# Weight and activation tiles begun 0 to 24 bytes inside buffers that are 32 bytes longer

## Chip, core and metric

The kernel runs on one core of one Trainium2 chip. The metric is the device time of one execution in microseconds (us), the median over runs. Before the change it is 1123.51 us, the median of three runs between 1121.23 and 1124.25 us.

## The reference

A trunk of two layers over 512 tokens of width 1024, all in float32. Layer 0 mixes tokens by stick-breaking attention (16 heads of 64), layer 1 by a gated MLP over chunks of 128 tokens; each is followed by a SwiGLU feed-forward of width 2816, and each of the four sub-layers is wrapped in RMSNorm before and after, with shift, scale and gate from a conditioning vector `c`.

```python
for i in range(DEPTH):                                   # 2 layers
    shift, scale, gate = ada_modulation(c, mix_ada_w[i], mix_ada_b[i])
    h = rms_norm(x, mix_pre_g[i]) * (1.0 + scale) + shift
    y = stick_breaking_mixer(...) if i == 0 else token_mixing_mixer(...)
    x = x + gate * rms_norm(y, mix_post_g[i])
    shift, scale, gate = ada_modulation(c, ffn_ada_w[i], ffn_ada_b[i])
    h = rms_norm(x, ffn_pre_g[i]) * (1.0 + scale) + shift
    y = (silu(h @ w_gate) * (h @ w_up)) @ w_down
    x = x + gate * rms_norm(y, ffn_post_g[i])
```

Nearly all of the arithmetic is dense matrix products with 1024 or 2816 rows of weights.

## The kernel before, in words

**Products.** Every float32 operand is split into a high part, rounded to the matmul format `float32r`, and a low part, the rest. A product is then three matmuls (`mm3`, lines 101 to 104): high by high, low by high, high by low. The split takes one ScalarE instruction (high) and one VectorE instruction (low); `split` is lines 109 to 114. All matmuls go through line 90, the transposes through line 98. Each matmul instruction shows in the profile twice: as a weight load (PEld, the stationary operand, 128 columns) and as the matmul (PE, the moving operand, 256 or 512 columns in nearly all of them, 128 in the transposes and the spatial gating).

**Which operand is which.** In the q/k projections, the u half of the gated MLP's input (`u`), and the gate and up products (`gu`, `r`) the weights are stationary (`wh`, `wl`) and the activations move (`hTh`, `hTl`, `Sh`, `Sl`). In the v projections (`v`), the output projections and the down products (`y`, `X`, `M`) the activations are stationary and the weights move.

**Gate and up.** Of the 22 blocks of 128 feed-forward columns, the first three run as plain products (`gu`), the other 19 by a scheme with seven half-size products in place of eight (`seven`, banks `r1` to `r3`), for which VectorE forms sums of weights (`f13`, `f24`) and of activations (`S`). The last down product does the same for part of its blocks (`M`, `X`).

**Where the tiles lie.** Two helpers hand out most of the buffers.

- `slot` (line 47) takes one of 28 buffers of 4,096 bytes per partition from the pool `s4`. Transposed activations, queries, keys, attention outputs, split activations, modulation rows, the rows of `x` that are loaded again, and some modulation weights (`rawada` where `slots=True`) all live there.
- `wtile` (line 151) takes a pair of buffers, `wh` and `wl`, from the pool `wpool`, with five buffers of 4,096 bytes for each, and later in turn from a sixth pair in `wpool2`.

Counted from the start of a partition, the pools lie one after the other in the order in which they are opened: the five `wh` buffers begin at byte 10,528 + 4,096 n, the five `wl` buffers at 31,008 + 4,096 n, the 28 slots at 65,088 + 4,096 n, and the sixth pair at 187,968 and 192,064. So, within 64 bytes, the ten buffers of `wpool` all begin at byte 32, and all slots and the sixth pair at byte 0; the unpadded buffers of the second weight block (`b21`) begin at byte 0 as well. The slices of them that a matmul reads lie at multiples of 512 bytes, which changes nothing in that. A tile's *phase* below is its start within 64 bytes. The raw weights land in buffers of another pool (`wraw`, `wraw2`), which are not touched by the change.

**Order.** The weights come as a written list (`stream`): each is loaded by SyncE's DMA queue, split, and used in that order. In the attention and in the first stage TensorE, VectorE and ScalarE are chained to the order in which the program writes their instructions; elsewhere a scheduler orders them by dependencies. Buffers are handed out as earlier tiles are released.

**Numbers of names.** `nm` (line 43) counts up one number for each name it makes; a tile's name ends in it.

Of the kernel before, what the change touches and what calls it, by code (L numbers as in the profile page):

```python
# [9 lines left out]
F32R = mybir.dt.float32r  # L10
# [3 lines left out]
P = 128  # L14
# [11 lines left out]
def trunk(ctx: ExitStack, tc: tile.TileContext, A: dict, out: bass.AP):  # L26
# [8 lines left out]
    s4 = ctx.enter_context(tc.tile_pool(name="s4", bufs=28))  # L35
# [3 lines left out]
    uid = [0]  # L39
# [3 lines left out]
    def nm(s):  # L43
        uid[0] += 1
        return f"{s}_{uid[0]}"

    def slot(dt, name, a=2, b=512):
        return s4.tile([P, a, b], dt, tag="s4", name=nm(name))

    def bank(name, tag="b"):  # L50
        return psum.tile([P, 512], F32, tag=tag, bufs=6 if tag == "b" else 2, name=nm(name))
# [82 lines left out]
    def wemit():  # L134
        n = len(got)
        src, a, b, key = stream[n]
        if len(raws) == n:
            wload()
        if src is None:
            if len(raws) == n + 1 < len(stream) and stream[n + 1][0] is None:  # L140
                wload()
            got.append(blocks(*raws[n]))
            return
        raw = raws[n]
        if dve.chain and len(raws) == n + 1 and stream[n + 1][0] is not None:
            wload()
        h, l = wtile(a, b)
        split(h[:], l[:], raw[:])
        got.append((h, l))

    def wtile(a, b):
        turn[0] = (turn[0] + 1) % sum(c for _, c in wpools)
        pool = wpools[0][0] if turn[0] < wpools[0][1] else wpools[1][0]
        return (
            pool.tile([P, a, b], F32R, tag="wh", name=nm("wh")),
            pool.tile([P, a, b], F32R, tag="wl", name=nm("wl")),
        )

    def block_loads(idx):
# [10 lines left out]
    def blocks(xr, yr):  # L170

        fp = fwork["pool"]
        x = wtile(KD, P)
        split(x[0][:], x[1][:], xr[:])
        b21 = [fp.tile([P, 4, P], F32R, tag=f"b21{i}", name=nm("b21")) for i in range(2)]
        split(b21[0][:], b21[1][:], yr[:, 0:4, :])
        f13 = fp.tile([P, KD, P], F32, tag="f13", name=nm("f13"))
        add = dve.tensor_tensor(
            f13[:].rearrange("p (a k) f -> p a (k f)", a=2),
            xr[:].rearrange("p (a k) f -> p a (k f)", a=2),  # L180
            yr[:, 4:8, :].rearrange("p (a k) f -> p a (k f)", a=1).to_broadcast([P, 2, 512]),
            ALU.add,
        )
        order(add, ready[0])
        t13 = wtile(KD, P)
        split(t13[0][:], t13[1][:], f13[:])
        f24 = fp.tile([P, KD, P], F32, tag="f24", bufs=1, name=nm("f24"))
        dve.tensor_tensor(f24[:, 0:4, :], f13[:, 0:4, :], xr[:, 4:8, :], ALU.add)
        dve.tensor_tensor(f24[:, 4:8, :], f24[:, 0:4, :], yr[:, 0:4, :], ALU.add)
        t24 = wtile(KD, P)  # L190
        split(t24[0][:], t24[1][:], f24[:])

        def half(t, i):
            return lambda k: (t[0][:, 4 * i + k, :], t[1][:, 4 * i + k, :])

        return {
            "B11": half(x, 0), "B22": half(x, 1), "B21": half(b21, 0),
            "T1": half(t13, 0), "T3": half(t13, 1), "T2": half(t24, 0), "T4": half(t24, 1),
        }
# [82 lines left out]
    cT, ident = pack[:, :KD], pack[:, KD : KD + P]  # L282
    cols = pack[:, KD + P :].rearrange("p (a b) -> p a b", a=2)
    x0 = [slot(F32, "x0", 1, 1024)[:, 0, :] for _ in range(NT)]
    for tt, xt in enumerate(x0):
        load(xt, A["x"][tt * P : (tt + 1) * P, :])
# [26 lines left out]
    class Bg:  # L313
# [24 lines left out]
        def run(self):  # L338
            for name, at, s, part in self.parts:
                acc = slot(F32, name, 1, D)[:, 0, :]  # L340
                ada[name, at] = acc
                nc.gpsimd.memset(acc, 0.0)
                load(acc[0:1, :], A["adab"][s, part], self.queue)
                for k in range(KD):
                    if self.slots:
                        raw = slot(F32, "rawada", 1, D)[:, 0, :]
                        load(raw, A["ada"][s, part, k])
                        yield
                    else:
                        self.ahead(1 + (k + 1 < KD or name != self.parts[-1][0]))  # L350
                        raw = self.raws.pop(0)
                    ada_stt(acc, raw, k)
                    if not self.slots:
                        yield
# [1171 lines left out]
```

## Time and profile before

| | |
|---|---|
| median of three runs | 1123.51 us (1121.23 to 1124.25) |
| the profiled execution: span from first to last instruction | 1122.0 us; its time around the span is not recorded apart |
| busy TensorE matmul / weight load | 1104.4 us / 993.9 us |
| busy VectorE / ScalarE / GpSimd | 903.3 / 603.4 / 39.8 us |
| matmuls | 7,318 |
| granted TensorE clock, mean | 0.995 |
| moved by DMA | 176.09 MB, 157 GB/s on average |

Durations of matmuls in the profile overlap: a new one starts before the one ahead of it has ended. What a matmul costs in a stretch without gaps is therefore not its duration but the time from its start to the next start, which this text calls its *step*.

### The profile page before, as it was taken

The page shows a single profiled execution, that of the slowest core. Times are in us where ns is not written, and L with a number is a line of the kernel's source. Part 1 is how long each engine was busy: PE and PEld are TensorE (multiplying, and loading weights), DVE is VectorE, ACT ScalarE, POOL GpSimd, SP SyncE. Part 2 cuts the span into 40 slices and gives each one's busy share as a digit, 9 for nine tenths or more (in the row PEclk, how much of TensorE's full clock was granted, in tenths as well). Part 3 has the DMA queues.
Part 4 walks back from the last instruction along what each step waited for, and adds up shares of the span by engine and source line. Part 5 has one row for each costly group of instructions (what it writes and reads, how often), then busy time and mean ns, then how long its engine had stood idle before and what let it go on. Part 6 is the DMA issues. An engine that isn't in the chain of part 4 may idle for free.

```text
span 1122.0 us, 18286 instructions
## 1 busy us (share of the span) xinstructions
PE 1104.4 (98%) x7318; PEld 993.9 (89%) x7318; DVE 903.3 (81%) x1161; ACT 603.4 (54%) x977; POOL 39.8 (4%) x71
## 2 busy tenths in 40 slices
PE   6999999999999999999999999999999999999997
PEld 5788878779999999988878988989999999989896
DVE  7777889759998988797587774759988988889986
ACT  7646767646655555552244634437555555556552
POOL 0220111000000000010000000000000000000000
PEclk9999999999999999999999999999999999999999
DMA  9676445353344444278874582333244444223223
GB/s 358 229 228 169 142 147 160 135 188 132 106 125 147 151 148 122 90 243 264 272 255 167 182 286 80 110 129 134 77 151 140 128 133 147 76 75 113 95 96 149
DMA packets 51298, 176.09 MB, mean 157 GB/s; under 512 B 5643, under 2 KB 6155, under 8 KB 50318
## 3 DMA queue, kind: packets, MB, share of 16 engines
q1 hardware_dynamic: 45166, 153.95, 42.0%
q0 software_dynamic: 6048, 20.98, 6.0%
q8 instruction: 57, 0.93, 0.3%
q14 instruction: 27, 0.22, 0.1%
HBM read 164.43 MB, written 8.39 MB: 154 GB/s over the span
## 4 chain that ended last, share of the span: by engine, by line
PE 88%; DMA 6%; DVE 3%; ACT 2%; issue 1%; SPq 0%; DVEq 0%; ACTq 0%
PE r L90 33%; PE y L90 12%; PE X L90 7%; PE v L90 7%; PE pqk L90 7%; PE gu L90 6%; PE u L90 4%; DMA rawada<-in_ada 3%; PE M L90 3%; PE z L90 2%; PE av L90 2%; PE tw L98 2%; DMA raw<-in_wdown 1%; DMA ada<-in_ada0w 1%; PE tp L98 1%; PE sv L90 1%
## 5 line engine op out<-in xcount | busy, mean ns | idle before, releaser
L64 ACT ACTIVATE wh<-raw 128x1024 fp32r<-128x1024 f32 (+1 forms) x112 | 117.0, 1051 | 138.3 <-PE y L90 45.6
L64 DVE TENSOR_TENSOR wl<-raw,wh 128x1024 fp32r<-128x1024 f32 (+1 forms) x112 | 135.0, 1211 | 59.4 <-ACT wh L64 57.9
L90 PE MATMUL r<-Sh,wh 128*128 128x256 f32 x608 | 170.2, 280 | 0.3 <-ACT e L64 0.3
L90 PE MATMUL r<-Sh,wl 128*128 128x256 f32 x608 | 170.4, 280 | 0.0
L90 PE MATMUL r<-Sl,wh 128*128 128x256 f32 x608 | 170.1, 280 | 0.0
L90 PE MATMUL y<-wh,as 128*128 128x512 f32 x480 | 154.0, 398 | 0.0
L64 DVE TENSOR_TENSOR wl<-f,wh 128x1024 fp32r<-128x1024 f32 x76 | 92.8, 1220 | 35.8 <-ACT wh L64 35.8
L64 ACT ACTIVATE wh<-f 128x1024 fp32r<-128x1024 f32 x76 | 80.7, 1061 | 67.9 <-PE r L90 64.8
L90 PEld LDWEIGHTS r<-Sh,wh 128*128 128x128 f32 x608 | 114.7, 189 | 0.5 <-ACT e L64 0.5
L90 PEld LDWEIGHTS r<-Sl,wh 128*128 128x128 f32 x608 | 114.6, 189 | 0.0
L90 PEld LDWEIGHTS r<-Sh,wl 128*128 128x128 f32 x608 | 114.6, 189 | 0.0
L90 PEld LDWEIGHTS y<-wh,as 128*128 128x128 f32 x480 | 90.7, 189 | 21.3
L90 PE MATMUL y<-wl,as 128*128 128x512 f32 x240 | 95.5, 398 | 0.0
L90 PE MATMUL r<-hTh,wh 128*128 128x256 f32 x304 | 88.8, 293 | 0.0
L90 PE MATMUL r<-hTl,wh 128*128 128x256 f32 x304 | 84.8, 279 | 0.0
L90 PE MATMUL r<-hTh,wl 128*128 128x256 f32 x304 | 80.1, 280 | 0.0
L90 PE MATMUL X<-wh,as 128*128 128x512 f32 (+1 forms) x272 | 76.2, 356 | 0.0
L64 ACT ACTIVATE e<-r 128x256 f32<-128x256 f32 x114 | 43.4, 382 | 51.9 <-PE r L90 51.7
L90 PEld LDWEIGHTS r<-hTh,wh 128*128 128x128 f32 x304 | 57.2, 188 | 5.1 <-DVE gu L64 0.9
L90 PE MATMUL r<-hTh,b 128*128 128x256 f32 x304 | 60.7, 282 | 0.0
L64 ACT ACTIVATE wh<-rawx 128x1024 fp32r<-128x1024 f32 x38 | 40.4, 1062 | 36.5 <-PE r L90 30.8
L90 PEld LDWEIGHTS r<-hTl,wh 128*128 128x128 f32 x304 | 57.3, 188 | 0.1
(240 smaller groups left out, 2842.6 us busy)
## 6 DMA issues: line engine op xcount, KB each, us to landing
rawada<-in_ada SPq DMA_DIRECT2D x56, 512.0 KB, 4.7
raw<-in_wdown SPq DMA_DIRECT2D x44, 512.0 KB, 4.0
rawy<-in_wy SPq DMA_DIRECT2D x38, 512.0 KB, 3.6
rawx<-in_wx SPq DMA_DIRECT2D x38, 512.0 KB, 4.3
rawada<-in_ada POOLq DMA_DIRECT2D x24, 512.0 KB, 4.5
raw<-in_wqk SPq DMA_DIRECT2D x16, 512.0 KB, 4.2
ada<-in_ada0w SPq DMA_DIRECT2D x7, 1026.0 KB, 11.2
raw<-in_wgu SPq DMA_DIRECT2D x12, 512.0 KB, 3.5
```

Source lines behind the costliest of these rows:

```text
L64: b = f(*a, **k)
L90: b = nc.tensor.matmul(o, l, r, start=start, stop=stop, skip_group_check=True)
L98: last_tp[0] = nc.tensor.transpose(o, i, ident)
```

## The change

Each buffer of `slot` and `wtile` gets 8 more float32 elements (32 bytes) per partition, and the tile begins `o` elements inside it, where `o` is 0, 2, 4 or 6 by a formula on the name's number. Nothing else is edited; the instructions, their shapes and their written order are the same.

```diff
+    PAD = 8
+
+    def shifted(pool, a, b, dt, tag, name):
+        t = pool.tile([P, a * b + PAD], dt, tag=tag, name=nm(name))
+        o = uid[0] * uid[0] // 3 % 4 * 2
+        return t[:, o : o + a * b].rearrange("p (a b) -> p a b", a=a)
+
     def slot(dt, name, a=2, b=512):
-        return s4.tile([P, a, b], dt, tag="s4", name=nm(name))
+        return shifted(s4, a, b, dt, "s4", name)
...
         return (
-            pool.tile([P, a, b], F32R, tag="wh", name=nm("wh")),
-            pool.tile([P, a, b], F32R, tag="wl", name=nm("wl")),
+            shifted(pool, a, b, F32R, "wh", "wh"),
+            shifted(pool, a, b, F32R, "wl", "wl"),
         )
```

Two things follow from the arithmetic alone. For a number u, `u * u // 3 % 4` depends only on u modulo 6 and is 0, 0, 1, 3, 1, 0: half of the tiles begin at byte 0 of their buffer, a third at byte 8, a sixth at byte 24, and none at byte 16. And buffers of 4,128 bytes no longer begin at the same phase: neighbours in a pool differ by 32 within 64 bytes, whatever `o` is.

## The prediction

> **What bounds the kernel now.** I read the clock first, then the busy shares, the chain that ended last, the stages, and at last the starts of single matmuls, because the change edits nothing but addresses.
>
> ```profile
> core 0: 1122.0 us, clock 0.995
> ```
> ```profile
> span 1122.0 us, 18286 instructions
> ...
> PE 1104.4 (98%) x7318; PEld 993.9 (89%) x7318; DVE 903.3 (81%) x1161; ACT 603.4 (54%) x977; POOL 39.8 (4%) x71
> ...
> PE 88%; DMA 6%; DVE 3%; ACT 2%; issue 1%; SPq 0%; DVEq 0%; ACTq 0%
> ```
>
> The clock is granted in full, matmuls are busy for 98% of the span, and 88% of the chain that ended last is TensorE. So the time is the sum of the matmuls' steps, plus some gaps. The span of 1122.0 us is 1.5 us below the median of 1123.51 and inside the three runs; I make the sum as a difference and take it from the median.
>
> ```profile
> core 0: us, PE busy (x) PEld busy (x) DVE busy (x) ACT busy (x) POOL busy (x), PEclk, DMA share, GB/s
> 296.00:480.00 184.00, 184.00 (x1536) 181.72 (x1535) 156.48 (x211) 98.97 (x166) 0.96 (x1) 1.00 0.41 130
> 480.00:580.00 100.00, 97.99 (x449) 80.14 (x448) 78.42 (x84) 37.76 (x56) 2.87 (x3) 0.98 0.81 263
> ```
>
> In the stage of the seven products VectorE is busy for 156.48 of 184 us, 85%: TensorE could go some per cent faster there before VectorE held it. From 480 to 580 us it is otherwise; a chain of loads of modulation weights, here its first and last, paces the end:
>
> ```profile
> 492.50 5.99 DMA rawada<-in_ada
> ...
> 544.21 4.88 DMA rawada<-in_ada
> ```
> ```profile
> PE adaps L90 <- ACT acch L64: 2.0, 1, 2.0
> ```
>
> TensorE waits there once, 2.0 us, for a row that hangs on those loads. What it gains ahead of that wait is given back.
>
> **Does a matmul's step depend on where its operands lie?** Four stretches without gaps, each by its first and last row or as one piece of the chain. The first has moving tiles at phase 0 and weights at phase 32 (256 columns), the second both at phase 0.
>
> ```profile
> 400.18 0.28 PE L90 MATMUL r<-Sl,wh 128*128 128x256 f32 x1
> 400.30 0.28 PE L90 MATMUL r<-Sh,wl 128*128 128x256 f32 x1
> 400.42 0.28 PE L90 MATMUL r<-Sh,wh 128*128 128x256 f32 x1
> 400.53 0.28 PE L90 MATMUL r<-Sl,wh 128*128 128x256 f32 x1
> ...
> 402.98 0.28 PE L90 MATMUL r<-Sl,wh 128*128 128x256 f32 x1
> ```
> ```profile
> 410.11 0.28 PE L90 MATMUL r<-Sh,wh 128*128 128x256 f32 x1
> ...
> 411.07 0.28 PE L90 MATMUL r<-Sh,wl 128*128 128x256 f32 x1
> ```
>
> 24 steps in 2.80 us are 116.7 ns; 8 steps in 0.96 us are 120.0 ns. These are the same products of the same block, and only the pair of weight buffers differs (`wpool`, then `wpool2`). Unrounded, the first stretch repeats 120, 113, 116, 117 ns, the second has 120 every time. Now 512 columns, first weights moving at phase 32 over activations at phase 0, then both at phase 0:
>
> ```profile
> 649.75 19.60 PE v L90 x84
> ```
> ```profile
> 999.22 0.62 PE L90 MATMUL X<-wh,as 128*128 128x512 f32 x2
> ...
> 1003.99 0.39 PE L90 MATMUL X<-wh,as 128*128 128x512 f32 x1
> ```
>
> 19.60/84 = 233.3 ns, against 21 steps in 4.77 us, 227.1 ns. So it does depend, and the two widths disagree: equal phases cost a 256-column matmul about 3 ns more, and a 512-column matmul 6 ns less. What runs beside each matmul is the weight load of the next, so I read this as two streams of reads that get in each other's way or don't, by their distance within 64 bytes.
>
> [...]
>
> **The change part by part.** Over the whole trace, the starts give 4,559 gapless steps of 256 columns with a mean of 117.7 ns (1,204 pairs at equal phases, 3,355 at 32 apart), and 1,948 of 512 columns with a mean of 232.7 ns (265 equal, 1,683 apart). Some of the groups they come from:
>
> ```profile
> L90 PE MATMUL r<-Sh,wl 128*128 128x256 f32 x608 | 170.4, 280 | 0.0
> L90 PE MATMUL y<-wh,as 128*128 128x512 f32 x480 | 154.0, 398 | 0.0
> ```
>
> Now both lengths change. Working out the new starts from the pools, with buffers taken in the same order as now, the distance between moving and stationary tile becomes: for 256 columns 20% equal, 19% 32 apart, 61% at 8, 16 or 24 either way; for 512 columns 18%, 15% and 67%. Most pairs get distances that this trace doesn't show.
>
> Bounds for those: below, the best step seen, 113.3 (the low one of the repeating four, 113 or 114) and 227.1; above, the worst seen, 120.0 and about 235 (the upper ones within the 84 above). Between them I take the middle. For 256 columns the repeating 120, 113, 116, 117 helps: these steps pass through different relative positions of the two streams, and their mean is 116.7, the middle of 113.3 and 120. Equal phases look like one position held for good, at the worst value. With distances that change from matmul to matmul nothing is held, so I expect the mean over positions: **256 columns: 116.7 − 117.7 = −1.0 ns, by 4,559 = −4.4 us.** For 512 columns the middle of 227.1 and 233.3 is 230.2: **230.2 − 232.7 = −2.5 ns, by 1,948 = −4.9 us.** Of these some 244 lie in the paced stretch (57 us from 492 to 549, at 233.3 ns each) and give back 244 × 2.5 ns = 0.6 us. Sum: −4.4 − 4.9 + 0.6 = **−8.7 us**.
>
> The other engines read and write the shifted tiles too. For VectorE the trace has a row: half of these sixteen have their input and output begun 8 bytes off a multiple of 32 (the second of two rows of 1,026 elements).
>
> ```profile
> L64 DVE SCALAR_TENSOR_TENSOR ada<-ada,scr x16: 1217/1220/1230, 10.9 to 45.3; 128x1026 f32<-128x1026 f32 x16
> ```
>
> Shortest to longest is 1217 to 1230 ns, so the shift costs VectorE at most 13 ns in 1,220, about 1%, and I take nothing: that would be lost in the 15% that it has free. ScalarE has no such row; at VectorE's 1% its 603.4 us grow by 6, and with 54% busy they lie beside matmuls. The loads into slots may pay for rows begun off 32 bytes. Two loads of 513 KB (one of them begun 8 bytes off) stand beside one of 512 KB in the same first 20 us:
>
> ```profile
> ada<-in_ada0w SPq DMA_DIRECT2D x2, 513.0 KB, 8.8
> ...
> raw<-in_wv SPq DMA_DIRECT2D x1, 512.0 KB, 9.4
> ```
>
> Not slower, so nothing for those either. If they did cost more, the cover is that slots are loaded ahead, except the last rows of `x`; none of the wide weight loads lands in a shifted buffer. No wait, no instruction and no queue position is added.
>
> **Where it lands.** 1123.5 − 8.7 = 1114.8 us. A measurement here can tell about 0.3% (3.4 us) from no change.
>
> **The rivals.**
>
> *No change.* Either new distances count in proportion between the two known points, or addresses matter little for other reasons. In proportion, 256 columns would cost the mean of 120.0 and 116.7, 118.35: +0.65 ns, +3.0 us; with −4.9 + 0.6 that is −1.3 us, **1122.2**. For it: the two widths react with opposite signs, so that a random mix cancels. Against it: the repeating four, whose mean is lower than such a mix.
>
> *Slower: a tile begun inside a 32-byte piece costs a further piece.* The steps 113.3, 116.7 and 120 lie 3.3 ns apart, eight columns of 4 bytes at this rate: as if the streams came in pieces of 32 bytes. A row that begins 8 or 24 bytes inside one touches one more. Where the 256-column step is held by weight load and moving stream alike (PEld 181.72 busy in 184), a shift of either would add 3.3 ns: 3,282 pairs have one, 10.8 us; for 512 columns only the moving one, 1,065 pairs, 3.5 us. −8.7 + 14.3 = +5.6 us, **1129.1**; on the proportional sum −1.3 + 14.3 = +13.0 us, 1136.5. It decides the sign from 8.7/14.3, some 60% of that price. For it: the even spacing of the steps. Against it: VectorE's row, which pays nothing for the same shift.
>
> [...]
>
> *Much faster: the streams hardly ever meet.* If 32 bytes and 0 are special because tiles at multiples of 32 fall into step, and everything else runs at the best step seen, 256 columns win 4.4 ns × 4,559 = 20 us and 512 columns 5.6 × 1,948 = 10.9 us: −30 us, 1093; half of it, since 40% of the pairs stay at 0 or 32, is about 1105. For it: 113 ns is reached, one time in four. Against it: no stretch holds it.
>
> **How the numbers follow.** The forecast (mean over positions) gets 0.42, no change 0.24, slower 0.24, much faster 0.10. The range reaches up between the two slower sums, to 1132, and down past the half of the best case, to 1101: outside lie most of what is left of the full best case and of the slower case on the proportional sum. Faster by over 0.3%: 0.42 + 0.10 = 0.52; within: 0.24; slower: 0.24.
>
> **What would show it.** In the changed kernel, the count and the durations of VectorE's and ScalarE's groups stay as they are, and the difference is in the steps alone. Right: `v`, `y` and `X` stretches at 228 to 232 ns instead of 233.3, `gu` and `r` stretches at 116 to 117.5, products from `wpool2` no longer at 120. The stage of the seven products (296 to 480) would shorten by about 1.5 us, and the wait of `adaps` for `acch` would grow. Wrong, and slower: 256-column steps at 118 to 121, or new longer steps whenever a tile is begun at 8 or 24. Wrong by another engine: VectorE's 1,220 ns or ScalarE's 1,060 ns grown, or TensorE waiting for either in the seven products.

## The result, and the profile after

The change made the kernel slower by 0.3%: 1125.6 us (median of five runs, 1124.73 to 1127.3) against 1122.09 us for the kernel before (five runs, 1119.92 to 1124.25), ratio 1.003 with a 95% interval of 1.0019 to 1.0042. The prediction was 1114.8 us; the time lies inside its range and on the other side of no change, at the edge of what can be told from it. The profiled execution of the changed kernel has a span of 1125.5 us and a time of 1127.3 us; the one of before has a span of 1122.0 us, so 3.5 us are to be found.

First the cores and the busy shares of the changed kernel.

```profile
core 0: 1125.5 us, clock 0.998
```
```profile
span 1125.5 us, 18286 instructions
...
PE 1109.6 (99%) x7318; PEld 1001.6 (89%) x7318; DVE 903.5 (80%) x1161; ACT 603.4 (54%) x977; POOL 39.8 (4%) x71
...
PE 85%; DMA 7%; DVE 5%; ACT 1%; issue 1%; SPq 0%; DVEq 0%; ACTq 0%
```

The instruction counts are the same, the mean granted clock is 0.998 against 0.995 (a difference that comes back below), and VectorE (903.3 before, 903.5 now) and ScalarE (603.4 twice) have not moved. Matmuls are busy for 5.2 us more and weight loads for 7.7 us more. The order of the 7,318 matmuls is unchanged too, so the place to look is the step.

Two products as whole pieces of the chain that ended last (start, us, what, number of matmuls), before and after; the `v` piece of before is in the prediction.

```profile
783.70 22.47 PE gu L90 x192
806.17 169.54 PE r L90 x1416
```
```profile
650.83 19.57 PE v L97 x84
...
785.17 22.90 PE gu L97 x192
808.07 170.98 PE r L97 x1416
```

The 192 matmuls of `gu` (256 columns) go from 22.47/192 = 117.0 to 22.90/192 = 119.3 ns, the 1,416 of `r`, small gaps included, from 119.7 to 120.7 ns. The 84 of `v` (512 columns) stay at 233: 19.57/84 = 233.0. Now the stretch of the seven products that the prediction read from 400 us on, and the `X` stretch near 1,002 us, in the changed kernel:

```profile
401.48 0.28 PE L97 MATMUL r<-Sh,wh 128*128 128x256 f32 x1
...
402.88 0.28 PE L97 MATMUL r<-Sh,wh 128*128 128x256 f32 x1
...
404.31 0.28 PE L97 MATMUL r<-Sh,wh 128*128 128x256 f32 x1
```
```profile
1002.47 0.62 PE L97 MATMUL X<-wh,as 128*128 128x512 f32 x2
...
1009.39 0.39 PE L97 MATMUL X<-wh,as 128*128 128x512 f32 x1
```

Twelve steps lie in each half of the first fence. In the first half the moving tiles (`Sh`, `Sl`) begin at a multiple of 32 bytes and `wh` 8 bytes inside one: 1.40/12 = 116.7 ns. In the second the moving tiles begin 24 and 8 bytes inside: 1.43/12 = 119.2 ns. That is the first hint at what was priced at nothing. The 30 steps of `X` take 6.92/30 = 230.7 ns, where this product took 227.1 before; its moving tiles begin at a multiple of 32 bytes, so here it is the distance alone that changed.

Summed over all starts of the two traces:

| gapless steps | before | after | difference |
|---|---|---|---|
| 256 columns | 117.66 ns x4,559 | 119.25 ns x4,573 | +1.59 ns, +7.3 us |
| 512 columns | 232.72 ns x1,948 | 233.05 ns x1,955 | +0.33 ns, +0.6 us |
| gaps between matmuls of these two widths | 26.5 us | 21.9 us | -4.6 us |

The sum is +3.3 us, the span's difference +3.5. So the steps by themselves lost 7.9 us, more than twice what the time shows; the rest came back in the gaps. In the changed kernel the 256-column steps sort by the start of their moving tile within 32 bytes: 118.49 ns at 0 (2,312 steps), 119.83 at 8 (1,393), 120.34 at 24 (868).

Much of the part that came back lies in the waits and behind one of them (engine and tile, released by; us in total, times, longest):

```profile
PE y L97 <- DVE G L71: 0.7, 1, 0.7
PE adaps L97 <- ACT acch L71: 0.6, 1, 0.6
PE r L97 <- DVE gu L71: 0.4, 1, 0.4
```
```profile
core 0: us, PE busy (x) PEld busy (x) DVE busy (x) ACT busy (x) POOL busy (x), PEclk, DMA share, GB/s
296.00:480.00 184.00, 183.59 (x1521) 182.18 (x1519) 155.60 (x210) 98.45 (x164) 0.00 (x0) 1.00 0.40 128
480.00:580.00 100.00, 98.77 (x464) 81.19 (x463) 78.15 (x84) 38.19 (x56) 3.83 (x4) 1.00 0.80 263
```

TensorE arrives 2.9 us later at `adaps`, which hangs on the paced loads and is ready 1.4 us later than before, and so waits 0.6 us there in place of 2.0. And the kernel before lost something more behind its longer wait, which the prediction did not see: in the profile the granted clock from 480 to 580 us is 0.98 (the row in the prediction) and here 1.00. In the kernel before it is 0.5 from 565.5 us on, for 3.4 us, and there seven matmuls of 512 columns take 427 ns and one 386, where the changed kernel takes 226 to 237. In the chain of the kernel before, the first five `y` matmuls behind the wait, then the next seven, of the same shape:

```profile
565.52 2.02 PE y L90 x5
...
569.17 1.63 PE y L90 x7
```

2.02/5 is 404 ns, 1.63/7 is 233 ns. By start times the changed kernel is 2.9 us behind at 551 us; the shorter wait gives back 1.5 us and the full clock as much, the wait for `G` takes 0.8 us, and at 613 us it is 0.8 us behind. From there the delay grows again to the end. In the stage of the seven products it gets through 1,521 matmuls in the window where the kernel before got through 1,536: 15 fewer, the opposite of the 1.5 us that this stage was to win.

### The profile page after: what moved, and what is told of

The parts are those of the page before. It is cut to its first block, busy times and chain, and to the rows that moved or that the text cites. A ratio compares the mean times of both kernels' runs of the same rounds, so it can differ in the third digit from the quotient of the medians.

```text
span 1125.5 us, 18286 instructions
## 1 busy us (share of the span) xinstructions
PE 1109.6 (99%) x7318; PEld 1001.6 (89%) x7318; DVE 903.5 (80%) x1161; ACT 603.4 (54%) x977; POOL 39.8 (4%) x71
## 4 chain that ended last, share of the span: by engine, by line
PE 85%; DMA 7%; DVE 5%; ACT 1%; issue 1%; SPq 0%; DVEq 0%; ACTq 0%
PE r L97 31%; PE y L97 12%; PE X L97 7%; PE v L97 7%; PE pqk L97 7%; PE gu L97 6%; PE u L97 4%; DMA rawada<-in_ada 4%; PE M L97 3%; PE z L97 2%; PE av L97 2%; PE tw L105 2%; DMA raw<-in_wdown 1%; DMA ada<-in_ada0w 1%; PE tp L105 1%
## 5 line engine op out<-in xcount | busy, mean ns | idle before, releaser
L71 ACT ACTIVATE wh<-raw 128x1024 fp32r<-128x1024 f32 (+1 forms) x112 | 117.0, 1051 | 137.5 <-PE y L97 37.4
L71 DVE TENSOR_TENSOR wl<-f,wh 128x1024 fp32r<-128x1024 f32 x76 | 92.8, 1221 | 36.8 <-ACT wh L71 36.8
L71 ACT ACTIVATE wh<-f 128x1024 fp32r<-128x1024 f32 x76 | 80.8, 1063 | 69.8 <-PE r L97 65.7
L71 ACT ACTIVATE wh<-rawx 128x1024 fp32r<-128x1024 f32 x38 | 40.4, 1063 | 37.5 <-PE r L97 31.4
```

The lines of the kernel that those rows point to most:

```text
L71: b = f(*a, **k)
```

## The experiments

The forecast had two ingredients: where the tiles lie to each other (*distance*: start of the moving tile less that of the stationary one), and where inside a piece of memory a tile begins (*offset*), which was priced at nothing. In the expectations theory 1 says that the offset of a tile costs and the longer buffers by themselves next to nothing; theory 2 that the longer buffers, which scatter the distances, cost it. Theory 3 came up after the first four kernels (e1, e2, e4, e5): distance counts within 256 bytes, not 64, as long as it is held. The step columns are means over all gapless steps of the width in one profiled execution.

| run | time, us | ratio to before, 95% | 256 columns, ns | 512 columns, ns |
|---|---|---|---|---|
| e1_longer_only | 1122.47 | 1.0009 [1.0000, 1.0018] | 118.23 | 232.00 |
| e2_all_8 | 1130.19 | 1.0079 [1.0066, 1.0093] | 120.36 | 233.62 |
| e14_all_16 | 1122.08 | 0.9993 [0.9973, 1.0013] | 117.87 | 231.48 |
| e13_slots_8 | 1129.83 | 1.0064 [1.0049, 1.0079] | 120.19 | 232.42 |
| e4_by_width | 1121.86 | 0.9993 [0.9981, 1.0006] | 118.29 | 231.36 |
| e6_spacer_224 | 1124.30 | 1.0011 [1.0000, 1.0022] | 119.92 | 227.97 |
| e8_by_width_256 | 1117.80 | 0.9949 [0.9936, 0.9963] | 117.56 | 228.09 |
| e10_held_64 | 1115.17 | 0.9946 [0.9931, 0.9961] | 116.79 | 228.13 |
| e11_held_more | 1114.07 | 0.9927 [0.9912, 0.9942] | 115.72 | 228.88 |

Three more kernels (e5, e9, e12) ran once each, so there are steps but no interval; they stand in their places below.

### The longer buffers alone

e1_longer_only is the change with every tile at byte 0 of its buffer; `shifted` takes the start as its last argument, here and for the slots:

```diff
+            shifted(pool, a, b, F32R, "wh", "wh", 0),
+            shifted(pool, a, b, F32R, "wl", "wl", 0),
```

> All 40 buffers are 32 bytes longer, as in the change, but every tile begins at byte 0 of its buffer: the mix of equal and 32-apart distances without any tile off a multiple of 32 bytes. Theory 1 (a moving tile that begins off a multiple of 32 bytes costs extra; the mix alone is nearly neutral): 256-column steps at about 118.2 ns (now 117.7), 512-column steps at about 231 (now 232.7), +2.5 and -3.3 us, so -1 us in all, ratio 0.999. Theory 2 (the mix of distances alone made the change slower, the offsets nothing): the same as the changed kernel, 256 columns at 119.2 ns, +3.5 us, ratio 1.003.

```profile
649.95 19.52 PE v L96 x84
...
783.81 22.76 PE gu L96 x192
```

Ratio 1.0009: next to nothing, as theory 1 has it; theory 2 fell. But the steps have changed: `gu` 22.76/192 = 118.5 against 117.0 ns, `v` 232.4 against 233.3. Over the whole trace 256 columns lose 0.57 ns (x4,560 = +2.6 us) and 512 columns win 0.72 ns (x1,948 = -1.4 us). And the two phases that stood apart in the kernel before, 117 and 120 ns, 227 and 233, are no longer told apart: each group of equal distance within 256 bytes has about the same mean (117.9 to 118.5 and 231.4 to 232.9 ns).

### The offset, all tiles alike

e2_all_8 has the same longer buffers, and every tile of `slot` and `wtile` begins 2 elements, 8 bytes, inside. All distances among them stay those of e1.

```diff
+        return shifted(s4, a, b, dt, "s4", name, 2)
...
+            shifted(pool, a, b, F32R, "wh", "wh", 2),
+            shifted(pool, a, b, F32R, "wl", "wl", 2),
```

> The same buffers, but every tile begins at byte 8: all distances between tiles as with the longer buffers alone, and every moving operand from them off a multiple of 32. Theory 1: in the changed kernel the 256-column steps with such a moving tile are 1.5 ns longer than the others (120.0 against 118.5), the 512-column ones 0.8; so 256 columns at about 120 ns and 512 at about 232, +7 and +1.5 us over the kernel with longer buffers alone, ratio to before about 1.007. Theory 2: the same time as with the longer buffers alone.

```profile
651.38 19.65 PE v L96 x84
...
786.20 23.12 PE gu L96 x192
```

Now `gu` takes 23.12/192 = 120.4 ns. Against e1 the offset costs 120.36 - 118.23 = 2.1 ns per 256-column matmul and 233.62 - 232.00 = 1.6 ns per 512-column matmul, and the ratio goes from 1.0009 to 1.0079. So the offset is a cost by itself.

### Which operand pays

e13_slots_8 begins only the slots 8 bytes inside and leaves the weights at byte 0. Slots move in most of the 256-column products and are stationary in most of the 512-column ones.

```diff
     def slot(dt, name, a=2, b=512):
+        return shifted(s4, a, b, dt, "s4", name, 2)
...
+            shifted(pool, a, b, F32R, "wh", "wh", 0),
+            shifted(pool, a, b, F32R, "wl", "wl", 0),
```

> Buffers 32 bytes longer, tiles of the slots begun at byte 8, weights at byte 0. Theory 1 (the moving operand alone pays for a start off 32): the 256-column steps whose moving tile is a slot at 120.3 as with all tiles at 8, the 512-column steps whose moving tile is a weight at 232.0 as with longer buffers alone, though their stationary tiles lie at 8; about +8 us against longer buffers alone, ratio to before 1.007. Rival (either operand pays): 512-column steps at 233.6 as well, and 256-column steps lower than 120.3 with only one of the two off.

```profile
651.15 19.49 PE v L96 x84
...
785.48 23.13 PE gu L96 x192
```

`gu`, whose activations move, pays the same as in e2: 23.13/192 = 120.5 ns. `v`, in which the same kind of tile is stationary, pays nothing: 19.49/84 = 232.0 ns. Over the trace: 256 columns 120.43 ns where the moving tile is off (4,122 steps) and 118.04 where only the stationary one is (455); 512 columns 234.04 (369) and 231.95 (1,531). **Only the moving operand pays.**

### The size of the piece

e14_all_16 is e2 with every tile 16 bytes inside, off a multiple of 32 but not of 16.

```diff
-        return shifted(s4, a, b, dt, "s4", name, 2)
+        return shifted(s4, a, b, dt, "s4", name, 4)
```

(and 4 in place of 2 for `wh` and `wl`).

> Buffers 32 bytes longer, every tile begun at byte 16. If the moving stream comes in pieces of 32 bytes: as with all tiles at 8, 120.4 and 233.6 ns, ratio 1.008. If the pieces are of 16 bytes: as with longer buffers alone, 118.2 and 232.0 ns, ratio 1.001.

```profile
648.83 19.46 PE v L96 x84
...
782.39 22.64 PE gu L96 x192
```

Nothing is paid: `gu` 22.64/192 = 117.9 ns, ratio 0.9993. So a start counts against a multiple of 16 bytes, not of 32 as in the prediction's rival; starts 4 or 12 bytes inside were not tried. A piece of 16 bytes holds four columns; at 227.1/512 = 0.44 ns a column, one more piece would by this estimate be some 1.8 ns, between the 1.6 and the 2.1 measured. That it is one more piece to read is argued by this and by the size, not shown.

### Distance within 64 bytes: refuted

If distance within 64 bytes decided, the best of both would be had by giving each product the phase that its width likes: 32 for 256 columns, 0 for 512. e4_by_width does it with weight buffers 64 bytes longer; the slots stay.

```diff
+        t = pool.tile([P, a * b + 16], dt, tag=tag, name=nm(name))
+        o = (phase - base) % 64 // 4
```

> Weights alone get buffers 64 bytes longer and begin at a phase chosen by use: weights of 512-column matmuls at phase 0 (equal to the slots), those of 256-column matmuls, also from the sixth pair and the second weight block, at phase 32. Every tile stays on a multiple of 32. If the distance between the moving tile and the weight load beside it sets the step: 256 columns at 116.8 ns throughout (some 1,150 steps gain 2.7 ns, 3 us), 512 columns at 227.3 (some 1,700 gain 5.8 ns, 10 us), of which some 2 us are given back in the stretch that loads pace: -11 us, ratio 0.990. If held distances are no better than mixed ones: between 0.998 and 1.002.

The expected 1% did not come: ratio 0.9993, with the steps of a mix, 118.29 and 231.36 ns. Yet in one stretch of this trace, from 277.04 to 278.08 us, the steps repeat 114, 116, 117, 120, 113 as in the kernel before. There the distances within 256 bytes are all 32; behind it they alternate (224, 224, 160) and the repeating is lost. e5_scan_256 is e4 with the weights of the seven products begun at 0, 8, ... 56 bytes in turn by block, the slots at 0.

```diff
+        PH256 = nblock[0] % 8 * 8
+        nblock[0] += 1
```

> The kernel of the phases by use, but in the blocks of the seven products the weights begin at phase 0, 8, 16 ... 56 in turn from block to block, over moving tiles at phase 0. Only weights lie off a multiple of 32 there. Theory 1 (only a moving tile off 32 costs): no phase is above 120 ns. Distance theory: 120 at phase 0, 116.7 at 32, and 8, 16 and 24 show whether the course between them is even (119.2, 118.4, 117.5), whether only equal phases are slow (117 at all others), or whether some distance holds 113.3.

All eight came out alike, 118.0 to 118.6 ns: no effect of distance while buffers of 4,160 bytes scatter it, and again none of an offset of the stationary tile.

### Distance within 256 bytes, held

Buffers of 4,096 bytes keep a distance modulo 256 from one matmul to the next. e6_spacer_224 leaves all buffers as before and puts 224 bytes between the first weight pool and the slots, which brings nearly every distance to 0 modulo 256.

```diff
+    spacer = adas.tile([P, 56], F32, name="spacer")
+    nc.gpsimd.memset(spacer[:], 0.0)
```

> The kernel before, with one piece of 224 bytes between the weight buffers of the first pool and the slots (and one GpSimd memset of it at the start). All buffers keep their 4,096 bytes; every distance between weights and slots that was 32 or 224 within 256 becomes 0, with none of them mixed. Theory 3 (the step is set by the distance within 256 bytes, and only where it is the same from matmul to matmul): 256-column steps at 119.7 ns nearly everywhere (some 3,350 of them +2.9 ns, +10 us), 512-column steps at 227 to 229 (some 1,680 at -5 ns, -8 us, of which about 1.5 given back in the stretch that loads pace): about +3 us, ratio 1.003, with two large changes of opposite sign inside. Rival (distance does nothing; longer buffers as such cost): nothing changes, 117.7 and 232.7 ns, ratio 1.000.

```profile
651.23 19.07 PE v L93 x84
...
784.06 23.03 PE gu L93 x192
```
```profile
PE adaps L93 <- ACT acch L67: 4.2, 1, 4.2
```

Hardly any change in the time, 1.0011, out of two large ones: `v` falls to 19.07/84 = 227.0 ns, `gu` rises to 23.03/192 = 119.9. No tile is off, no buffer longer; 224 bytes moved both widths at once. And the faster 512-column stage runs into the paced loads: the wait at `adaps` is 4.2 us in place of 2.0, and 6.8 us at half the clock go with it in place of 3.4.

e8_by_width_256 then gives each width its own: weight buffers of `wpool` are 256 bytes longer, begun so that 512-column products lie at distance 0 and 256-column ones at 32, modulo 256. To make room, the small tiles `ab` moved to another pool, here and in the kernels below.

```diff
+    B512, B256, BM = 40, 32, 48
...
+        t = pool.tile([P, a * b + 64], dt, tag=tag, name=nm(name))
+        return t[:, o : o + a * b].rearrange("p (a b) -> p a b", a=a)
```

> The phases by use once more, but the weight buffers of the first pool are 256 bytes longer (the sixth pair and the second weight block stay as they are), so that distances within 256 bytes no longer change from tile to tile: weights of 512-column matmuls at distance 0 to the slots, those of 256-column matmuls at 32. Theory 3: 512-column steps at 227 to 229 instead of 231.4 (and 232.7 before), 256-column steps at 116.7 from the first pool and 120 from the sixth pair and the second block as before: -8 us against before, less 1.5, ratio 0.994. Rival (the stretch of steady steps seen in the kernel with 64-byte longer buffers was chance): 118.3 and 231.4 again, ratio 0.999.

```profile
649.07 19.06 PE v L90 x84
```
```profile
PE adaps L90 <- ACT acch L64: 3.9, 1, 3.9
```

Ratio 0.9949, as expected: 512 columns at 228.09, 256 columns as before. e9_scan_256 varies the distance by block in steps of 32 while it holds it within a block.

```diff
+        B256 = (160 - nblock[0] % 8 * 32) % 256 // 4
```

> The same kernel, but the blocks of the seven products take distances 0, 32, 64 ... 224 within 256 bytes in turn from block to block, and the weights of the first down product and of the v half go through the same eight distances from tile to tile. Theory 3: each distance holds its own steady step, 256 columns at 120 for 0 and 116.7 for 32; whether some distance holds 113.3 (256) or less than 227 (512) isn't foretold. If only the distance within 64 counts, all even multiples of 32 give 120 and 227, all odd ones 116.7 and 233. Rival: all distances alike, 118 and 231.

Three blocks of it, at distances 0, 64 and 96, each by its first and last row:

```profile
293.27 0.28 PE L90 MATMUL r<-hTh,wh 128*128 128x256 f32 x1
...
301.90 0.28 PE L90 MATMUL r<-hTh,wh 128*128 128x256 f32 x1
...
316.44 0.28 PE L90 MATMUL r<-Sh,wh 128*128 128x256 f32 x1
...
321.89 0.28 PE L90 MATMUL r<-hTh,wh 128*128 128x256 f32 x1
...
327.78 0.28 PE L90 MATMUL r<-Sh,wh 128*128 128x256 f32 x1
...
330.65 0.28 PE L90 MATMUL r<-Sh,wh 128*128 128x256 f32 x1
```

72 steps in 8.63 us are 119.9 ns, 48 in 5.45 are 113.5, 24 in 2.87 are 119.6. All eight, where the distance had been the same for some steps:

| distance modulo 256 | 0 | 32 | 64 | 96 | 128 | 160 | 192 | 224 | mean |
|---|---|---|---|---|---|---|---|---|---|
| 256 columns, ns | 119.9 | 116.8 | 113.7 | 119.9 | 118.5 | 117.8 | 117.8 | 118.2 | 117.8 |
| 512 columns, ns | 227.5 | 233.3 | 228.8 | 233.7 | 233.3 | 234.2 | 233.8 | 232.2 | 232.1 |

The kernel before stood mostly on 32 and 0 (256 columns; 353 steps, of `M` and `X`, on 224) and on 224, 32 and 0 (512). The period is not 128, since 0 and 128 differ in both widths, and nothing shows a longer one: in the e10 stretch at 113.3 ns below, the distances modulo 1,024 go through 64, 320, 576 and 832, and the steps stay. At 256 columns the values for 64 and 192 turned out otherwise in later kernels, as the last experiments show. The means over all eight come near what the scattered kernels show: each distance's step weighted by how often it comes in e1 gives 117.9 and 232.1 ns (118.23 and 232.00 measured), in e14 117.8 and 232.1 (117.87 and 231.48), in e4 118.2 and 230.7 (118.29 and 231.36).

e12_fine_scan does the same in steps of 8 bytes around 64, with the stationary tile of the 256-column products off and the moving tile of the 512-column ones.

```diff
+        B256 = (160 - (40 + nblock[0] % 8 * 8)) // 4
```

> Distances at 8-byte steps: 40 to 96 from block to block in the seven products (there only the weights lie off 32, as the stationary operand), and 0 to 56 from tile to tile for the weights of the first down product and of the v half (there the moving operand lies off 32). Theory 1: stationary off 32 costs nothing of its own, so the course from 32 (116.8) over 64 (113.7) to 96 (119.9) is smooth or stepwise; moving off 32 costs: 8, 16 and 24 are all longer than both 0 (227.3) and 32 (233.3) would have between them, by 1 to 3 ns. Rival (offsets as such do nothing): 512-column steps between 227 and 233.5 at 8, 16 and 24.

256 columns: 119.9, 116.9, 116.9, 116.6, 117.8, 118.1, 114.4, 119.8 ns at 40, 48, ... 96; 512 columns: 227.4 at 0, 231.5 to 233.5 at 8 to 56. Eight bytes are enough to change the step: from 119.8 at 96 to 114.4 at 88 (256 columns), and from 227.4 at 0 to over 231 at every other distance tried (512), also at 16, where e14 shows no cost of the offset. At 64 bytes the mean is 116.6 here and 113.7 in e9. Whether a moving tile 8 bytes off costs anything on top in this held arrangement isn't to be told here, since its distance changes with its offset.

### Can it be put to use?

e10_held_64 is e8 with the 256-column products at distance 64; e11_held_more also brings the sixth pair to a better distance by 64 bytes in front of it.

```diff
-    B512, B256, BM = 40, 32, 48
+    B512, B256, BM = 40, 24, 56
```

> The phases by use with 256-byte longer weight buffers, but weights of 256-column matmuls at distance 64 (in the last product, where weights move, 64 the other way round), as the scan showed 113.7 ns held there; 512-column ones stay at distance 0. Theory 3: some 3,330 steps of 256 columns at 113.9 instead of 116.9, -10 us against the kernel with distance 32: ratio to before 0.986. Rival: with steps that short the seven products run into VectorE, which is busy 85% of that stage: TensorE's waits for VectorE grow there and less than half of it arrives, ratio 0.991 or more.

```profile
274.19 0.28 PE L90 MATMUL gu<-hTh,wh 128*128 128x256 f32 x1
...
287.79 0.28 PE L90 MATMUL gu<-hTh,wh 128*128 128x256 f32 x1
...
779.24 0.28 PE L90 MATMUL gu<-hTl,wh 128*128 128x256 f32 x1
...
793.25 0.28 PE L90 MATMUL gu<-hTh,wh 128*128 128x256 f32 x1
```

```diff
-    B512, B256, BM = 40, 24, 56
+    B512, B256, BM = 32, 16, 48
...
+    spacer = spool.tile([P, 16], F32, name="spacer")
+    nc.gpsimd.memset(spacer[:], 0.0)
```

> As the kernel with distance 64, and 64 bytes stand between the slots and the sixth pair with what lies behind it, so that 256-column matmuls from there go from distance 0 to 192 (117.8 in the scan instead of 119.9) and 512-column ones from 0 to 64 (229 to 231 instead of 227.2). One 16-byte pair of scalars shares a buffer to make room. Theory 3: 1,080 steps -2 ns, some 210 steps +3 ns: -1.6 us against the kernel with distance 64, ratio to before 0.985. Rival (those steps don't repeat, since their neighbours are at another distance): no difference.

```profile
PE adaps L90 <- ACT acch L64: 3.5, 1, 3.5
...
PE r L90 <- DVE gu L64: 1.8, 8, 0.4
```

Some 40% and 50% of what was expected came: 0.9946 and 0.9927 in place of 0.986 and 0.985. Two reasons are in the traces. First, the same kind of product at the same distance of 64 has two patterns: 120 steps of e10 in 13.60 us are 113.3 ns in the first feed-forward, 119 steps in 14.01 us are 117.7 in the second, and a stretch keeps its pattern until something disturbs it (one of e10 goes from 113 to 118 ns behind a single step of 131 ns). Over all 3,333 steps of e10 at this distance the mean is 115.7 ns, not the 113.9 expected. Distance 192 has the two patterns as well: 117.8 ns in e9, but 114.7 on average over the 1,068 steps of e11 there, 776 of them at 115 ns or less. So a value of the scan can be one of two that its distance has. Second, faster products run into other limits: in e11 the wait at `adaps` (3.5 us, and 3.4 us at half the clock around its end) and VectorE's `gu` (eight waits, 1.8 us). e11 at 1114.07 us is the fastest version found, 0.73% under the kernel before.

## Why the prediction was wrong

**What failed first: "I expect the mean over positions", with 116.7 and 230.2 ns.** That scattered distances give about a mean over positions fits the runs; the mean was taken over the wrong positions. The repeating 120, 113, 116, 117 was read as a pass through all positions, but it is one held distance of eight (32), and a good one; 0, the other one known, is one of the two worst. Over eight the mean is 117.8, and e1 measured 118.23. For 512 columns the middle between the two known values, 230.2, assumed that good and bad positions are equally many: only two of eight (0 and 64) are good, and the mean is 232.1. So the terms of -4.4 and -4.9 us were, by e1, +2.6 and -1.4 us. The rival *No change* had the 256 columns nearly right with its proportional 118.35, but by luck: it is the middle of the values at 0 and 32 alone.

**What failed second: the tiles' offset on TensorE at nothing.** It costs 2.1 ns (256 columns) and 1.6 ns (512) for a moving tile begun 8 bytes off a multiple of 16. In the changed kernel 49% of the 256-column steps and 55% of the 512-column ones have such a moving tile. Half of the step from e1 to e2 (0.70%) is 0.35%, and with e1's 0.09% that makes 0.44%; 0.30% was measured, within what the intervals of the three leave open. The time lies inside the forecast's range only because that range reached up to cover the rivals; the sign of the forecast was wrong. The rival *Slower* had this mechanism in part: right that the moving stream pays for a start inside a piece; wrong on the piece (16 bytes, not 32: 117.87 and 231.48 ns in e14) and on the price (2.1, not 3.3, which is some seven columns at 116.7/256 ns each and not the eight it took), and wrong that the weight load pays too (e13: 118.04 against e1's 118.23). It used VectorE's row as evidence against itself, and that row was no evidence on TensorE:

```profile
L71 DVE SCALAR_TENSOR_TENSOR ada<-ada,scr x16: 1215/1218/1230, 11.1 to 45.1; 128x1026 f32<-128x1026 f32 x16
```

**What was right.** Steps depend on addresses: 512 columns at equal phase 227, 256 columns 120 ns. With nothing but addresses edited, products of one shape took 119.9, 113.5 and 119.6 ns in three blocks of e9, at distances 0, 64 and 96. VectorE and ScalarE pay nothing. The row above is of a tile that the change does not shift, in both kernels; these two are of weight tiles that it does, half of them begun 8 or 24 bytes inside, and take 1,221 and 1,063 ns on average against 1,220 and 1,061 before:

```profile
L71 DVE TENSOR_TENSOR wl<-f,wh 128x1024 fp32r<-128x1024 f32 x76 | 92.8, 1221 | 36.8 <-ACT wh L71 36.8
L71 ACT ACTIVATE wh<-f 128x1024 fp32r<-128x1024 f32 x76 | 80.8, 1063 | 69.8 <-PE r L97 65.7
```

The loads into slots pay nothing either. The 513 KB loads that the prediction took for this land in buffers outside the slots; the rows of `x` land in slots, 13 of the 20 now begun 8 or 24 bytes inside, and take 6.6 and 5.5 us from issue to landing against 6.5 and 5.8 before:

```profile
x<-xd SPq DMA_DIRECT2D x12, 512.0 KB, 6.6
x<-in_x SPq DMA_DIRECT2D x8, 512.0 KB, 5.5
```

The paced stretch gives back what happens ahead of it, only with the other sign: from 551 to 613 us 2.1 of the 2.9 us lost by then came back, so that the profile shows 3.5 us instead of more. The wait that the prediction named gave back 1.5 us; the full clock behind it gave as much, which the prediction did not have, and the wait for `G` took 0.8 us again. The signs named beforehand were clear: "256-column steps at 118 to 121" came, `v` at 228 to 232 did not, and the wait of `adaps` shrank.

**What stays open.** Why the steps at distances 64 and 192 have two patterns. How the two streams meet in the memory: that the weight load of the next matmul is the other stream is argued from the dependence on the distance between the two operands, but no kernel ran with the load taken away. And why in e1 a matmul at distance 0 takes 118.3 ns and not its held 119.9: in a scattered stretch each distance shows the common mean, so the place of the matmuls ahead counts too.

## What to carry to other kernels

Where float32r matmuls run without gaps, each beside a weight load as here, a buffer's size and a pool's start are part of the kernel's speed (0.5 to 0.7% in e8, e10 and e11): keep the moving operand's start on a multiple of 16 bytes (8 off cost 2.1 and 1.6 ns a step in e2), and keep buffer sizes a multiple of 256 so that the distance between moving and stationary tile stays held and can be chosen (113.7 to 119.9 ns at 256 columns in e9); a pad of 32 bytes gives up the choice (118.23 ns in e1). Before taking a middle or a mean over cases that the trace doesn't show, ask how many cases there are and which of them the trace happens to sit on. And vary such a price by block inside one kernel: e9 alone gave sixteen values, though later kernels showed that two of them (64 and 192 at 256 columns) are one of two patterns.

## What the runs showed of the hardware

- The step of a float32r matmul beside the next weight load depends on the distance of the moving and the stationary tile modulo 256 bytes, if held: 113.7 to 119.9 ns (256 columns), 227.5 to 234.2 ns (512 columns) in e9, and the two widths like different distances (64 with 113.7 ns, 0 with 227.5 ns).
- Scattered distances give 117.9 to 118.3 and 231.4 to 232.0 ns (e1, e4, e14), near the mean over the held ones.
- With scattered distances, a moving tile begun 8 bytes off a multiple of 16 costs 2.1 ns (256) or 1.6 ns (512) in e2; 16 bytes off a multiple of 32 costs nothing (e14: 117.87 and 231.48 ns, against 118.23 and 232.00 in e1); a stationary tile's offset costs nothing (e13: 118.04 and 231.95 ns).
- One distance can have two steady patterns, 113.3 and 117.7 ns, for products of one shape (distance 64 in e10).
- The granted clock can fall to 0.5 around the end of a TensorE wait: in the profiles it did so for 3.4 or 6.8 us in seven of the nine kernels whose wait at `adaps` is 1.9 us or longer, and there in none of the five others.
